# Differential attention in a hybrid trunk layer: queries and keys transposed once in fp32, duplicated by on-chip transfers, and split after the transposition

## The chip, the cores and the metric

The kernel runs on one core of a Trainium2 chip. The metric is the device time of one execution in microseconds. Five engines work side by side: TensorE (PE in the profile, its weight loads PEld), VectorE (DVE), ScalarE (ACT), GpSimd (POOL) and SyncE (SP), which here only issues transfers (DMAs). Each engine takes its instructions strictly in order, and an instruction that waits holds back everything behind it on its engine. [...]

## The reference, cut to what matters

One layer, 640 tokens (512 latent and 128 context tokens), width 1024: a SwiGLU half-step, then token mixing (differential attention beside an mLSTM), then a second half-step. The attention has 8 heads. Each has two components `c` of 64 features for queries and keys and 128 features for values:

```python
dq = rmsnorm(dq.reshape(B, T, DA_HEADS, 2, DA_HEAD_DIM), p['g_qn'][l])
dk = rmsnorm(dk.reshape(B, T, DA_HEADS, 2, DA_HEAD_DIM), p['g_kn'][l])
q_att = rope_2d(dq)
keys = jnp.concatenate([rope_2d(dk), k_ctx.astype(dk.dtype)], axis=1)
s = jnp.einsum('bqhcd,bkhcd->bhcqk', qi.astype(jnp.float32), kf) * scale
pr = jax.nn.softmax(s, axis=-1)
w = pr[:, :, 0] - lam * pr[:, :, 1]
return jnp.einsum('bhqk,bkhv->bqhv', w, vf)
```

The latent queries see 512 latent keys and 256 cached ones, the context queries see the 128 context keys. Everything is fp32; the inputs are given and the result is compared in fp32.

## The kernel before, in words

**Split products.** TensorE multiplies fp32 data in a faster reduced format, `float32r`. To keep the precision, every operand is split into a high part (the value rounded to `float32r`) and a low part (the value minus the high part), and products of high and low are summed. The high part is a Copy on ACT (`act`, line 51), the low part a subtraction on DVE (`tt`, line 54).

**The scores of a head.** A query component has only 64 features, so a contraction over 128 partitions has room for two copies. The query operand `qT` holds for each component the high part on one half of the partitions and the low part on the other half. The key operands `kH` and `kL` hold the high and the low part of the keys, the same on both halves. Then `qT` times `kH` plus `qT` times `kL` is the full product (`Head.scores`, line 708). The cached keys come from HBM in this layout already (`ck`, lines 1698 to 1700) and are only split.

**Getting there, before.** After the projections queries and keys lie token-major (`q_tok`, `k_tok`: 128 tokens on the partitions, 5 blocks of tokens), and the features have to come onto the partitions. `pack_queries` (1664) splits token-major into slots of 64 columns (high 0, low 0, low 1, high 1) in `qpk`, with one ACT and one DVE instruction; `pack_keys` (1672) lays the high part of the keys out twice in `kpk` with two ACT instructions. `queries` (1689) then turns `qpk` with ten TensorE transpositions (5 blocks by 2 components, `turn_features`, line 1679, through the `float32r` identity `identr`), which ACT copies from PSUM into `qT`; it makes the low part of the keys, also twice, in `kp2` (two DVE subtractions) and loads and splits the cached keys. `keys(0)` turns `kpk` (ten more, emptied by DVE), `keys(1)` turns `kp2` (ten more, emptied by ACT). So a head takes 30 transpositions, and the 8 heads take 240.

**Order of the work.** TensorE runs in program order (`mm`, `tr`, lines 74 to 78). Inside `with written()` ACT and DVE instructions are chained in the order written; all others, and the transfers issued by `nc.sync.dma_start`, are placed by a planner that simulates the timeline. Between the steps of a head, `fill.units(n)` puts projection work on TensorE. Such a unit is 24 matmuls of 256 columns or, in heads 1 to 5, half of a wide pair: 12 matmuls of 512 columns, two units after each other into the one PSUM bank `wide` (line 1366, `bufs=1`), which ACT empties with two instructions after the second half. The other PSUM tiles share four banks, tag `mm`. A head has ten such units, so the halves fall alike in each wide head: the last three units before the next head are a second half, a first half and a second half.

**A head in the loop** (lines 2103 to 2154). For each block of queries `qi` = 0 to 4: `scores(qi)`, `turn(qi-1)` (transposes the softmax weights, `ps_wT`), `soft(qi)` (two Exp on ACT), one unit, `mix(qi)` (DVE), `values(qi-1)` (`ps_o`), perhaps a second unit. At `qi == 3` the next head is packed. After the last block: `turn(4)`, `N.queries()`, a unit, `H.values(4)`, `finish_norm` (normalises the head's output), `N.keys(0)`, a unit, `N.keys(1)`, `fill.ahead()` (loads and begins to split a later granule of weights), a unit; then the next head. `H.finish` (transposes the output, `ps_aT`, in fp32 through `ident`, and stores it) runs inside the next head. Before head 0 the same steps run between eleven units (2068 to 2081), followed by `gate_rows` (1428), which prepares the mLSTM gates and stores two tiles `QA`, `QB` that `gate_load` and `gate_cols` (1509, 1512) bring back during head 1.

**Buffers.** The tag `pk` (two buffers of 5 KB a partition) holds rope scratch, `qpk`, `kpk` and `kp2`; the tag `asq` (one buffer of 2.5 KB) holds `ck`, `asq`, `aT` and `QQ`.

Of the kernel before, what the change touches and what calls it, by code (L numbers as in the profile page):

```python
# [18 lines left out]
NS = 512  # L19
# [12 lines left out]
def tile_trunk(ctx: ExitStack, tc: tile.TileContext, a: dict):  # L32
# [17 lines left out]
    def act(*args, **kw):  # L50
        return placed(nc.scalar.activation(*args, **kw))  # L51
# [1344 lines left out]
    mix = ctx.enter_context(ExitStack())  # L1396
    gq_p = mix.enter_context(tc.tile_pool(name="mlgate", bufs=1))
    ident = load(gq_p, [128, 128], a["ident"], name="ident")
    identr = gq_p.tile([128, 128], F32R, name="identr")
    vec.tensor_copy(identr, ident)  # L1400
    cols = gq_p.tile([128, 5, 4, 8], F32, name="cols")
    decay = gq_p.tile([128, 64, 5], F32, name="decay")

# [24 lines left out]
    def gate_rows(gt, ps):  # L1428
        b_g, m0 = of_rows

        def row(name):
            return gt.tile([64, T], F32, name=name)

        fg, ig = row("fg"), row("ig")
        for hf in range(2):
            cs = half(hf)
            p = ps[:, 512 * hf : 512 * hf + HALF]
            act(fg[:, cs], p[0:64], AF.Identity, bias=b_g[0:64])
            act(ig[:, cs], p[64:128], AF.Identity, bias=b_g[64:128])
# [12 lines left out]
        yield  # L1452
        tt(vec, u, ig, b, ALU.subtract)

        A, M = keep, lf
        vec.memset(A, 0.0)
        vec.tensor_copy(A[0:32, 128:512:128], b[0:32, 127:511:128])
        vec.tensor_copy(A[32:64, 127:511:128], b[32:64, 128:512:128])
        vec.memset(M, 0.0)
        yield  # L1460
        for d0, fl in ((0, False), (32, True)):
            r = slice(d0, d0 + 4)
            for c0, c1, init in ((0, 512, m0[r, 0:1]), (512, 640, 0.0)):
# [24 lines left out]

        yield
        QA = gt.tile([128, T], F32, name="QA")  # L1490
        QB = gt.tile([128, T], F32, name="QB")
        vec.tensor_copy(QA[0:64], u)

        def r3(t):
            return t.rearrange("p (c t) -> p c t", c=5)

        tt(vec, r3(e), r3(u), Ml[:, :, None].to_broadcast([64, 5, 128]), ALU.subtract)
        act(QA[64:128], e, AF.Exp)
        tt(vec, r3(ig), r3(nM), MP[:, :, None].to_broadcast([64, 5, 128]), ALU.add)
        act(QB[0:64], ig, AF.Exp)  # L1500
        tt(vec, b, nM, b, ALU.subtract)
        ts(b, b, 87.0, ALU.min)
        act(QB[64:128], b, AF.Exp)
        nc.sync.dma_start(out=qq_dram[:, 0, :], in_=QA)
        nc.sync.dma_start(out=qq_dram[:, 1, :], in_=QB)

    Q_at = [None]

# [145 lines left out]
    class Head:  # L1654
# [2 lines left out]
            self.pr, self.h = divmod(hd, 2)  # L1657
            self.s = {}

        def pack(self):  # L1660
            self.pack_queries()
            self.pack_keys()

        def pack_queries(self):

            hs = slice(self.h * 128, (self.h + 1) * 128)
            qv = q_tok[self.pr][:, :, hs].rearrange("p t (c d) -> p t c d", c=2)
            self.qpk = ap.tile([128, 5, 4, 64], F32R, tag="pk", name="qpk", bufs=2)
            act(self.qpk[:, :, 0::3, :], qv, AF.Copy)
            tt(vec, self.qpk[:, :, 1:3, :], qv, self.qpk[:, :, 0::3, :].bitcast(F32), ALU.subtract)  # L1670

        def pack_keys(self):
            hs = slice(self.h * 128, (self.h + 1) * 128)
            kv = self.kv = k_tok[self.pr][:, :, hs].rearrange("p t (c d) -> p t c d", c=2)
            self.kpk = ap.tile([128, 5, 4, 64], F32R, tag="pk", name="kpk", bufs=2)
            for i in range(2):
                self.at_act = act(self.kpk[:, :, i::2, :], kv, AF.Copy)

        def turn_features(self, pk, dst, key, ev):
            for i0, n in ((0, 2), (2, 2), (4, 1)):  # L1680
                p = psum.tile([128, 2, 2, 128], F32R, tag="mm", name="ps_qkT")
                for i in range(n):
                    flat = pk[:, i0 + i].rearrange("p s d -> p (s d)")
                    for c in range(2):
                        tr(p[:, c, i, :], flat[:, 128 * c : 128 * c + 128], identr)
                o = 768 if key and i0 == 4 else i0 * 128
                ev(dst[:, :, o : o + n * 128].rearrange("p c (i t) -> p c i t", i=n), p[:, :, :n, :].bitcast(F32))

        def queries(self):
            self.qT = ap.tile([128, 2, T], F32R, tag="qT", name="qT")  # L1690
            self.kH = ap.tile([128, 2, 896], F32R, tag="kH", name="kH")
            self.kL = ap.tile([128, 2, 896], F32R, tag="kL", name="kL")
            self.ao = ap.tile([128, 5, 128], F32, tag="ao", name="ao")
            self.turn_features(self.qpk, self.qT, False, lambda o, i: setattr(self, "at_q", act(o, i, AF.Copy)))
            self.kp2 = ap.tile([128, 5, 4, 64], F32R, tag="pk", name="kp2", bufs=2)
            for i in range(2):
                self.at_vec = tt(vec, self.kp2[:, :, i::2, :], self.kv, self.kpk[:, :, i::2, :].bitcast(F32), ALU.subtract)
            ck = load(ap, [128, 2, 256], a["cache_kd"][:, self.hd], tag="asq", name="ck")
            act(self.kH[:, :, 512:768], ck, AF.Copy)
            tt(vec, self.kL[:, :, 512:768], ck, self.kH[:, :, 512:768].bitcast(F32), ALU.subtract)  # L1700

        def keys(self, part):
            if part == 0:
                self.turn_features(self.kpk, self.kH, True, lambda o, i: vec.tensor_copy(o, i))
            else:
                self.turn_features(self.kp2, self.kL, True, lambda o, i: act(o, i, AF.Copy))

        def scores(self, qi):
            s = ps_s.tile([128, 1536], F32, tag="sc", name="sc")
# [358 lines left out]
    heads[0].pack()  # L2068
    fill.units(3)
    heads[0].queries()  # L2070
    fill.units(2)
    heads[0].keys(0)
    fill.units(2)
    heads[0].keys(1)
# [7 lines left out]
    def aside(hd, qi, part):  # L2082
# [7 lines left out]
                rotate()  # L2090
        elif qi != 3:
            rotate()
        if part == 1 and hd == 1 and qi in (1, 2):
            gate_load(qi - 1)
        if part == 0 and hd == 1 and qi in (2, 3):
            gate_cols()

    two, one = (1, 1), (1, 0)
# [4 lines left out]
    for hd in range(8):  # L2103
        H = heads[hd]
        odd = hd % 2
        for qi in range(5):
            n = UNITS[hd][qi]
            with written():
# [14 lines left out]
            if qi == 3 and hd < 7:  # L2123
                while odd and rotate():
                    pass
                with written():
                    heads[hd + 1].pack()
            aside(hd, qi, 1)
            if (hd, qi) == (0, 2):
                begin_pools()  # L2130
# [8 lines left out]
        with written():  # L2139
            H.turn(4)  # L2140
        if hd < 7:
            N = heads[hd + 1]
# [563 lines left out]
```

## Time and profile before

| | |
|---|---|
| device time, median of 3 runs | 1804.94 us (1804.79 to 1805.13) |
| the profiled execution: its time, and its span from first to last instruction | 1804.37 us, 1802.4 us |
| TensorE busy | 1778.2 us, 99% of the span |
| DVE busy, ACT busy | 1349.6 us (75%), 899.0 us (50%) |
| granted TensorE clock | 1.000 |
| the attention, head 0's first unit to the last head's end | about 654 to 1056 us |
| in that stretch: TensorE, DVE, ACT busy; DMA share | 398.7, 277.7, 228.4 of 402.1 us; 0.27 |
| one wide head (2 to 5) | 45.8 to 45.9 us |

How to read it: times are microseconds from the start of the span. A busy TensorE is not one at its peak, since matmuls overlap: the next one starts before the last one has ended. What an instruction costs TensorE is therefore the distance from its start to the next start, and not its duration. In a timeline row the number behind the start is the duration of the whole group, `xN` the instructions in it, and brackets show idle time of that engine ahead of it with what ended it. Names of tiles have their buffer numbers left out; all ACT instructions of the helper carry line 51, all DVE subtractions line 54, the transpositions line 78.

### The profile page before, as it was taken

The page shows a single profiled execution, that of the slowest core. Times are in us where ns is not written, and L with a number is a line of the kernel's source. Part 1 is how long each engine was busy: PE and PEld are TensorE (multiplying, and loading weights), DVE is VectorE, ACT ScalarE, POOL GpSimd, SP SyncE. Part 2 cuts the span into 40 slices and gives each one's busy share as a digit, 9 for nine tenths or more (in the row PEclk, how much of TensorE's full clock was granted, in tenths as well). Part 3 has the DMA queues.
Part 4 walks back from the last instruction along what each step waited for, and adds up shares of the span by engine and source line. Part 5 has one row for each costly group of instructions (what it writes and reads, how often), then busy time and mean ns, then how long its engine had stood idle before and what let it go on. Part 6 is the DMA issues. An engine that isn't in the chain of part 4 may idle for free.

```text
span 1802.4 us, 29657 instructions
## 1 busy us (share of the span) xinstructions
PE 1778.2 (99%) x11950; PEld 1712.3 (95%) x11950; DVE 1349.6 (75%) x2162; ACT 899.0 (50%) x1579; POOL 40.8 (2%) x72
## 2 busy tenths in 40 slices
PE   8999999999999999999999999999999999999998
PEld 6999999999999999888889998899999999999998
DVE  6879887576888858777775637876768888896485
ACT  5654544332655556565655546562326545544432
POOL 0000000100000000000000000000000000000010
PEclk9999999999999999999999999999999999999999
DMA  8364565978235543222222335665642455557992
GB/s 330 110 199 162 193 241 205 360 220 279 90 120 194 187 147 96 78 72 75 72 87 98 111 121 196 201 245 190 227 164 77 143 167 190 207 176 274 355 311 82
DMA packets 144923, 317.85 MB, mean 176 GB/s; under 512 B 10577, under 2 KB 106577, under 8 KB 133009
## 3 DMA queue, kind: packets, MB, share of 16 engines
q1 hardware_dynamic: 133410, 270.20, 43.7%
q0 software_dynamic: 10688, 43.13, 7.4%
q10 hardware_dynamic: 688, 2.63, 0.4%
q8 instruction: 94, 1.54, 0.3%
q14 instruction: 43, 0.35, 0.1%
HBM read 243.77 MB, written 72.15 MB: 175 GB/s over the span
## 4 chain that ended last, share of the span: by engine, by line
PE 85%; DVE 7%; DMA 4%; ACT 2%; issue 1%; SPq 0%; ACTq 0%; DVEq 0%
PE ps_f L75 48%; PE ps_p L75 15%; PE ps_t L75 10%; PE sc L75 3%; PE ps_o L75 2%; PE ps_n L75 2%; DVE ww L54 2%; DMA raw_a<-in_w_ada_k 1%; PE ps_wT L78 1%; PE ps_u L75 1%; PE ps_qkT L78 1%; DMA raw<-in_w2b 1%; DVE junk L814 1%; DMA a_raw<-aT_dram 1%; DMA P<-nm_dram 1%
## 5 line engine op out<-in xcount | busy, mean ns | idle before, releaser
L75 PE MATMUL ps_f<-S,ww 128*128 128x320 f32 x2400 | 387.2, 309 | 4.4 <-ACT u L51 1.9
L75 PEld LDWEIGHTS ps_f<-S,ww 128*128 128x128 f32 x2400 | 359.7, 188 | 8.7 <-DVE ww L54 4.6
L54 DVE TENSOR_TENSOR ww<-raw,ww 128x2048 fp32r<-128x2048 f32 (+1 forms) x73 | 163.9, 2245 | 66.0 <-ACT ww L51 65.9
L75 PE MATMUL ps_f<-hm,ww 128*128 128x320 f32 x1176 | 185.7, 309 | 0.1
L75 PEld LDWEIGHTS ps_f<-hm,ww 128*128 128x128 f32 x1176 | 175.7, 188 | 0.4 <-DVE ww L54 0.3
L51 ACT ACTIVATE ww<-raw 128x2048 fp32r<-128x2048 f32 (+1 forms) x73 | 136.8, 1875 | 59.7 <-DVE raw L54 40.3
L54 DVE TENSOR_TENSOR raw<-raw 128x1024 f32<-128x1024 f32 x186 | 160.8, 864 | 2.4
L75 PE MATMUL ps_f<-hm,wB 128*128 128x320 f32 x1008 | 161.5, 309 | 0.0
L75 PE MATMUL ps_t<-wH,hH 128*128 128x256 f32 (+1 forms) x440 | 151.6, 345 | 1.0 <-DVE x L57 0.9
L75 PE MATMUL ps_p<-hH,wH 128*128 128x320 f32 x480 | 150.9, 314 | 1.6 <-DVE num L54 1.6
L75 PEld LDWEIGHTS ps_f<-hm,wB 128*128 128x128 f32 x1008 | 151.3, 188 | 0.0
L75 PE MATMUL ps_p<-hH,wL 128*128 128x320 f32 x480 | 148.3, 309 | 0.0
L75 PE MATMUL ps_p<-hL,wH 128*128 128x320 f32 x480 | 148.3, 309 | 0.0
L75 PE MATMUL ps_t<-wH,hL 128*128 128x256 f32 (+1 forms) x440 | 146.4, 333 | 0.9 <-DVE hL L54 0.9
L75 PE MATMUL ps_t<-wL,hH 128*128 128x256 f32 (+1 forms) x440 | 146.3, 333 | 0.0
L51 ACT ACTIVATE u<-ps_f 128x320 f32<-128x320 f32 x129 | 55.7, 432 | 154.6 <-PE ps_f L75 154.5
L54 DVE TENSOR_TENSOR wL<-raw,wH 128x2048 fp32r<-128x2048 f32 x37 | 84.6, 2288 | 25.9 <-ACT wH L51 25.9
L51 ACT ACTIVATE wH<-raw 128x2048 fp32r<-128x2048 f32 (+1 forms) x45 | 75.4, 1681 | 49.7 <-PE ps_p L75 40.3
L54 DVE TENSOR_TENSOR wB<-raw,wB 128x1024 fp32r<-128x1024 f32 x64 | 78.0, 1219 | 26.6 <-ACT wB L51 26.6
L814 DVE CUSTOM_DVE_ANT_0 junk<-raw_a,csil 128x1024 bf16<-128x1024 f32 (+1 forms) x76 | 92.6, 1218 | 2.1 <-DMA raw_a<-in_w_ada_c 1.6
L75 PEld LDWEIGHTS ps_t<-wH,hL 128*128 128x128 f32 x440 | 83.6, 190 | 9.8 <-DVE hL L54 1.1
L75 PEld LDWEIGHTS ps_t<-wH,hH 128*128 128x128 f32 x440 | 83.5, 190 | 9.4 <-ACT nsq L51 1.1
(311 smaller groups left out, 3569.7 us busy)
## 6 DMA issues: line engine op xcount, KB each, us to landing
g_dram<-g SPq DMA_DIRECT2D x44, 640.0 KB, 7.5
raw_a<-in_w_ada_c POOLq DMA_DIRECT2D x38, 512.0 KB, 5.1
g_dram<-g SPq DMA_DIRECT2D x24, 480.0 KB, 8.6
raw<-in_w1b SPq DMA_DIRECT2D x11, 1024.0 KB, 4.9
raw<-in_w3b SPq DMA_DIRECT2D x11, 1024.0 KB, 6.4
raw<-in_w1a SPq DMA_DIRECT2D x10, 1024.0 KB, 4.9
raw<-in_w3a SPq DMA_DIRECT2D x10, 1024.0 KB, 6.2
hm<-g_dram SPq DMA_DIRECT2D x7, 1280.0 KB, 13.3
```

The source lines that it names most:

```text
L51: return placed(nc.scalar.activation(*args, **kw))
L54: return placed(eng.tensor_tensor(out=out, in0=in0, in1=in1, op=op))
L75: tc.keep_in_program_order(nc.tensor.matmul(*args, **kw))
L78: tc.keep_in_program_order(nc.tensor.transpose(*args, **kw))
L814: placed(vec.tensor_tensor_reduce(out=junk, in0=raw, in1=self.csil[:, v, :], op0=ALU.mult, op1=ALU.add, scale=1.0, scalar=0.0, accum_out=m ...
```

## The change

Queries and keys are turned once, whole and unsplit, in fp32. `turned` replaces the packing and `turn_features`: five transpositions through the fp32 identity `ident` for a head's 128 columns (both components together: component 0 lands on partitions 0 to 63, component 1 on 64 to 127), in two PSUM tiles, which ACT copies into an SBUF tile `t`. Four transfers from SBUF to SBUF then write each component's 64 partitions onto both halves of a tile `both` (160 KB each, 64 partitions by 2560 bytes, all issued by SP). Only then is the data split, feature-major: `queries` copies all of `qd` into `qT` as the high part and overwrites partitions 64 to 127 with the low part; `keys` makes `kH` and `kL` from the cached keys (part 0), the latent keys (1) and the context keys (2).

```diff
-    identr = gq_p.tile([128, 128], F32R, name="identr")
-    vec.tensor_copy(identr, ident)
...
+        def turned(self, tok):
             hs = slice(self.h * 128, (self.h + 1) * 128)
+            t = ap.tile([128, T], F32, tag="asq", name="qk_t")
+            for i0, n in ((0, 4), (4, 1)):
+                p = psum.tile([128, 4, 128], F32, tag="mm", name="ps_qkT")
                 for i in range(n):
+                    tr(p[:, i, :], tok[:, i0 + i, hs], ident)
+                act(t[:, i0 * 128 : (i0 + n) * 128], p.rearrange("p a b -> p (a b)")[:, : n * 128], AF.Copy)
+            both = ap.tile([128, 2, T], F32, tag="pk", name="qk_d", bufs=2)
+            for r in range(2):
+                for c in range(2):
+                    nc.sync.dma_start(out=both[64 * r : 64 * r + 64, c, :], in_=t[64 * c : 64 * c + 64])
+            return both
+        def turn_queries(self):
+            self.qd = self.turned(q_tok[self.pr])
+        def turn_keys(self):
+            self.kd = self.turned(k_tok[self.pr])
+        def load_cache(self):
+            self.ck = load(ap, [128, 2, 256], a["cache_kd"][:, self.hd], tag="ck", name="ck")
...
+            self.at_q = act(self.qT, self.qd, AF.Copy)
+            r = slice(64, 128)
+            tt(vec, self.qT[r], self.qd[r], self.qT[r].bitcast(F32), ALU.subtract)
+        def keys(self, *parts):
+            for n in parts:
+                c0, c1 = ((512, 768), (0, 512), (768, 896))[n]
+                v = (self.ck, self.kd[:, :, 0:NS], self.kd[:, :, NS:T])[n]
+                act(self.kH[:, :, c0:c1], v, AF.Copy)
+                self.at_vec = tt(vec, self.kL[:, :, c0:c1], v, self.kH[:, :, c0:c1].bitcast(F32), ALU.subtract)
```

In the loop the steps lie so. At `qi == 3`, where the next head was packed, its queries are turned; at `qi == 4`, behind `values(3)`, its keys. After `turn(4)` come `N.queries()` and `N.keys(0)`, a unit, `H.values(4)`, `N.keys(1, 2)`, then `finish_norm` and the other two units with no transposition between them. All these are now inside `written()`, except that the transfers are placed by the planner.

```diff
                 with written():
-                    heads[hd + 1].pack()
+                    N.turn_queries()
+                N.load_cache()
+            if qi == 4 and hd < 7:
+                with written():
+                    N.turn_keys()
...
-            N.queries()
+            with written():
+                N.queries()
+                N.keys(0)
             fill.units(n[0])
             with written():
                 H.values(4)
+                N.keys(1, 2)
             H.finish_norm()
-            N.keys(0)
             fill.units(n[1])
-            N.keys(1)
```

Ahead of head 0 the two turns come first, then three units, `queries`, `keys(0, 1, 2)`, four units, and the rest as before. Three smaller edits go with it: `ck` gets a buffer of its own and `asq` is used by `t` instead; `gate_rows` works in place and stores four half tiles instead of `QA` and `QB`; and `gate_load` and `gate_cols` move from head 1 to heads 2 and 4, since they use `asq`.

More of the change, by code (lines that the diff above doesn't have):

```diff
@@ L1489, in gate_rows @@
         yield
-        QA = gt.tile([128, T], F32, name="QA")
-        QB = gt.tile([128, T], F32, name="QB")
-        vec.tensor_copy(QA[0:64], u)
         def r3(t):
             return t.rearrange("p (c t) -> p c t", c=5)
+        nc.sync.dma_start(out=qq_dram[0:64, 0, :], in_=u)
         tt(vec, r3(e), r3(u), Ml[:, :, None].to_broadcast([64, 5, 128]), ALU.subtract)
-        act(QA[64:128], e, AF.Exp)
+        act(e, e, AF.Exp)
+        nc.sync.dma_start(out=qq_dram[64:128, 0, :], in_=e)
         tt(vec, r3(ig), r3(nM), MP[:, :, None].to_broadcast([64, 5, 128]), ALU.add)
-        act(QB[0:64], ig, AF.Exp)
+        act(ig, ig, AF.Exp)
+        nc.sync.dma_start(out=qq_dram[0:64, 1, :], in_=ig)
         tt(vec, b, nM, b, ALU.subtract)
         ts(b, b, 87.0, ALU.min)
-        act(QB[64:128], b, AF.Exp)
-        nc.sync.dma_start(out=qq_dram[:, 0, :], in_=QA)
-        nc.sync.dma_start(out=qq_dram[:, 1, :], in_=QB)
+        act(b, b, AF.Exp)
+        nc.sync.dma_start(out=qq_dram[64:128, 1, :], in_=b)
     Q_at = [None]
@@ L1658, in __init__ @@
             self.s = {}
[L1660 to L1664, printed above, removed]
+        def turned(self, tok):
             hs = slice(self.h * 128, (self.h + 1) * 128)
[L1667 to L1681, printed above, removed]
-                for i in range(n):
[L1683 to L1687, printed above, removed]
+            t = ap.tile([128, T], F32, tag="asq", name="qk_t")
@@ L1693, in queries @@
             self.ao = ap.tile([128, 5, 128], F32, tag="ao", name="ao")
[L1694 to L1706, printed above, removed]
+            self.at_q = act(self.qT, self.qd, AF.Copy)
[7 more added lines that the diff above has]
+                self.at_vec = tt(vec, self.kL[:, :, c0:c1], v, self.kH[:, :, c0:c1].bitcast(F32), ALU.subtract)
         def scores(self, qi):
@@ L2067, in tile_trunk @@
     gt = gates.enter_context(tc.tile_pool(name="gates", bufs=1))
-    heads[0].pack()
+    heads[0].load_cache()
+    heads[0].turn_queries()
+    heads[0].turn_keys()
     fill.units(3)
     heads[0].queries()
[L2071 to L2074, printed above, removed]
+    heads[0].keys(0, 1, 2)
+    fill.units(4)
     with tc.issue_after(heads[0].at_vec.ins), tc.issue_after(heads[0].at_q.ins):
@@ L2092, in aside @@
             rotate()
-        if part == 1 and hd == 1 and qi in (1, 2):
-            gate_load(qi - 1)
-        if part == 0 and hd == 1 and qi in (2, 3):
+        if (qi, part) == (1, 1) and hd in (2, 4):
+            gate_load(hd // 2 - 1)
+        if (qi, part) == (2, 0) and hd in (2, 4):
             gate_cols()
@@ L2105, in tile_trunk @@
         odd = hd % 2
+        N = heads[hd + 1] if hd < 7 else None
         for qi in range(5):
@@ L2141, in tile_trunk @@
         if hd < 7:
-            N = heads[hd + 1]
-            N.queries()
+            with written():
+                N.queries()
+                N.keys(0)
             fill.units(n[0])
```

## The prediction

> **What bounds the kernel now.** I read the page first, then busy time by stage, then TensorE's timeline where one head hands over to the next.
>
> ```profile
> span 1802.4 us, 29657 instructions
> ...
> PE 1778.2 (99%) x11950; PEld 1712.3 (95%) x11950; DVE 1349.6 (75%) x2162; ACT 899.0 (50%) x1579; POOL 40.8 (2%) x72
> ...
> PE 85%; DVE 7%; DMA 4%; ACT 2%; issue 1%; SPq 0%; ACTq 0%; DVEq 0%
> ...
> 825.80:871.70 45.90, 45.80 (x267) 39.22 (x266) 31.39 (x47) 26.47 (x57) 0.00 (x0) 1.00 0.24 74
> ...
> 653.90:1056.00 402.10, 398.73 (x2650) 362.41 (x2649) 277.66 (x423) 228.44 (x477) 0.00 (x0) 1.00 0.27 87
> 1056.00:1250.00 194.00, 190.30 (x1168) 177.93 (x1167) 136.45 (x394) 106.02 (x265) 2.65 (x5) 1.00 0.60 208
> ```
>
> TensorE bounds the whole program and this stage too: 398.73 of 402.10 us in the attention. The third and fourth busy times of a stage row are DVE and ACT, and both have room. So what shortens TensorE's row of starts shortens the time, unless a wait takes the place. The end of head 3 (wide units) shows the row:
>
> ```profile
> 853.34 1.50 PE L75 MATMUL ps_o<-v_tok,wT 128*128 128x128 f32 x12
> 854.60 0.36 PE L75 MATMUL sc<-kH,qT 128*128 128x256 f32 x1
> ...
> 859.18 1.50 PE L75 MATMUL ps_o<-v_tok,wT 128*128 128x128 f32 x12
> 860.51 0.27 PE L78 MATMUL ps_wT<-ident,p 128*128 128x128 f32 x1
> 860.54 1.05 PE L78 MATMUL ps_qkT<-identr,qpk 128*128 128x128 f32 x10
> 861.42 0.46 PE L75 MATMUL ps_t<-wH,hH 128*128 128x512 f32 x1
> ...
> 864.03 0.39 PE L75 MATMUL ps_t<-wH,hL 128*128 128x512 f32 x1
> 864.26 0.38 PE L75 MATMUL ps_o<-v_tok,wT 128*128 128x128 f32 x2
> 864.40 1.05 PE L78 MATMUL ps_qkT<-identr,kpk 128*128 128x128 f32 x10
> 865.28 0.46 PE L75 MATMUL ps_t<-wH,hH 128*128 128x512 f32 x1
> ...
> 868.11 0.96 PE L78 MATMUL ps_qkT<-identr,kp 128*128 128x128 f32 x10
> 868.91 0.46 PE L75 MATMUL ps_t<-wH,hH 128*128 128x512 f32 x1
> ...
> 871.75 0.39 PE L75 MATMUL sc<-kH,qT 128*128 128x512 f32 x1
> ...
> 875.94 0.71 PE L78 MATMUL ps_aT<-ident,ao 128*128 128x128 f32 x5
> 876.41 0.48 PE L75 MATMUL ps_t<-wH,hH 128*128 128x512 f32 x1
> ```
>
> **Removed: 30 transpositions a head.** From start to next start the three groups take 861.42 − 860.54 = 0.88, 865.28 − 864.40 = 0.88 and 868.91 − 868.11 = 0.80, so 2.56 us a head and 20.5 us for eight.
>
> **Added: 10 transpositions a head in fp32.** The row for five fp32 transpositions of this shape is `ps_aT`: 876.41 − 875.94 = 0.47 us. Two groups make 0.94 us a head, 7.5 us in all. Net on TensorE: −13.0 us.
>
> **Given back: the bank of the wide units.** In heads 1 to 5 the first unit after `turn(4)` ends a wide pair, and the next one needs the same single bank. ACT empties it thus:
>
> ```profile
> 861.12 1.36 ACT L51 ACTIVATE qT<-ps_qkT 128x512 fp32r<-128x512 f32 x3
> 864.46 0.38 ACT L51 ACTIVATE k_tok<-ps_t 128x256 f32<-128x256 f32 x1 [1.97 <-PE ps_t L75]
> 864.74 0.38 ACT L51 ACTIVATE q_tok<-ps_t 128x256 f32<-128x256 f32 x1
> ```
>
> The pair ends at 864.03 + 0.39 = 864.42, the bank is empty at 864.74 + 0.38 = 865.12, and the next unit can start near 865.16. Before, the ten `kpk` transpositions fill just that time. After the change only `ps_o` (0.14 us) lies there, so the unit would be ready at 864.40 and waits 0.76 us. Five such places: +3.8 us. This assumes that ACT is free then. In `written()` order ACT has the two copies of the turned keys (0.60 and 0.28), `wT`, the Copy into `qT` (1.27) and the cached keys (0.64) ahead, 3.1 us, less the overlaps between neighbours; counted from X, the start of the keys' transpositions (860.4 on the clock above, where `ps_o` of block 3 is through), they run from X + 0.6 to about X + 3.5. The pair ends at X + 0.47 + 0.10 (`wT`) + 2.84 (a unit, 861.42 to 864.26) + 0.16 (its last matmul's overhang, 864.42 − 864.26) = X + 3.6. It fits, barely.
>
> ```profile
> L51 ACT ACTIVATE wT<-ps_wT 128x512 f32<-128x512 f32 x32 | 19.1, 597 | 52.8 <-PE ps_wT L78 52.6
> ...
> L51 ACT ACTIVATE wT<-ps_wT 128x128 f32<-128x128 f32 x8 | 2.2, 278 | 18.9 <-PE ps_wT L78 18.9
> ...
> L51 ACT ACTIVATE rope<-k_tok 128x1280 f32<-128x1280 f32 x3 | 3.8, 1273 | 0.0
> ...
> L51 ACT ACTIVATE kH<-ck 128x512 fp32r<-128x512 f32 x8 | 5.1, 638 | 1.0 <-DMA ck<-in_cache_kd 0.7 <-PE sc L75 0.3
> ...
> L51 ACT ACTIVATE rope<-k_tok 128x1024 f32<-128x1024 f32 x3 | 3.2, 1069 | 0.9 <-DVE k_tok L54 0.9
> ...
> L54 DVE TENSOR_TENSOR k_tok<-k_tok,rope 128x1024 f32<-128x1024 f32 x3 | 3.7, 1219 | 0.0
> ...
> L54 DVE TENSOR_TENSOR k_tok<-k_tok,qky 128x1280 f32<-128x1280 f32 x3 | 4.5, 1492 | 0.1
> ```
>
> **Covered: stalls at `qi == 4`.** TensorE now waits there, in most heads, for the mixed weights of block 3 and for a bank behind the packing on ACT (waits in us in total, times, longest):
>
> ```profile
> PEld ps_wT L78 <- DVE p L57: 2.1, 6, 0.9
> ...
> PEld ps_t L75 <- ACT stage L51: 1.0, 4, 0.3
> ...
> PEld ps_t L75 <- ACT q_tok L51: 0.5, 2, 0.3
> ```
>
> The queries' transpositions (0.47 us) come to lie ahead of `scores(4)`, the keys' ahead of `turn(4)`, so the first 2.1 us are work instead of waiting; and ACT has 0.9 us of copies at `qi == 3` where it had three packings, so I take 1 of the other 1.5. Together −3 us (bounds: 0 and −3.6).
>
> **The transfers.** No row of the trace shows one from SBUF to SBUF, or on 64 partitions. Nearest rows, with the KB moved and the median from issue to landing:
>
> ```profile
> mq_dram<-stage SPq DMA_DIRECT2D x9, 160.0 KB, 1.9
> ...
> mkT<-mk_dram SPq DMA_DIRECT2D x2, 640.0 KB, 3.9
> ...
> mqT<-mq_dram SPq DMA_DIRECT2D x1, 640.0 KB, 8.9
> ...
> 881.31 0.33 SPq L97 DMA_DIRECT2D ck<-in_cache_kd  x1
> ```
>
> Let L be the time from the first issue of a turn to its last landing. Issues take 0.33 us each. Four transfers side by side give 3 × 0.33 + 1.9 = 2.9; 640 KB as one gives 3.9; bounds 2.9 and 8.9; I take 3.9, the same bytes on an idle queue. The stage uses 0.27 of the DMA engines, and at this boundary SP issues little else. The keys' `t` is ready at X + 0.6 + 0.9, so they land at X + 1.6 + L = X + 5.5. `kH` takes ACT 1.07 and `kL` DVE 1.22 us: ready at X + 7.9 with the semaphores. TensorE reaches the next `scores(0)` at X + 3.6 + 0.7 + 2 × 2.84 = X + 10.0. Hidden, with 2 us to spare; its cover is the two units behind `values(4)`. The single `asq` buffer is a second limit: the keys' copy at X + 0.6 needs the queries' transfers out of it, which start about 4.5 us before X: turned behind `ps_o` of block 2 at 854.6, copied until 855.9. With L = 3.9 that holds too.
>
> [...]
>
> ACT and DVE otherwise lose work: DVE gives up `qpk`, `kp`, and the emptying of `kH`, ACT the packings and two emptyings of `ps_qkT`; what they gain is the six rows above and a 1.5 us subtraction for `qT`. I cost this at nothing; TensorE's units hide it. So too the gate stores and the moved `gate_load`.
>
> **Ahead of head 0.** The removed groups lie there too. New: the four `mm` banks all go to the turns at once, and ACT has this in front:
>
> ```profile
> 654.00 1.92 ACT L51 ACTIVATE wH<-raw 128x2048 fp32r<-128x2048 f32 x1 [1.06 <-PE ps_f L75]
> 655.82 0.41 ACT L51 ACTIVATE g_out<-ps_f 128x320 f32<-128x320 f32 x1
> ```
>
> The transpositions would end near 654.9, and the first copy starts at 655.9, so the first unit gets its bank at 655.9 + 0.6 = 656.5: +1.6 us (0 if the planner puts the copies first, +4 if the banks of the last gate products and the keys' copy come late as well).
>
> **Sum.** −13.0 + 3.8 − 3.0 + 1.6 = −10.6 us. 1804.37 − 10.6 = 1793.8 on the profiled execution's time, which is 0.57 below the median of the runs: 1794.3 us. With the bounds of the terms this case spans 1790 to 1799.
>
> **Rivals.** (a) *More of it arrives*: the wide bank or the start costs nothing. Without the +3.8 and the +1.6: about 1789. For it: the planner may order anew; against it: the bank's row is firm.
>
> (b) *ACT is held by the keys' transfer; slower.* If the planner expects the keys' landing before the wide pair's end, it puts their Copy into `kH` ahead of the two copies that empty the bank. Then ACT stands until X + 5.5, copies 1.07, empties 0.66: the unit starts at X + 7.2 instead of X + 4.3, 2.9 us at five places, 14.5 us: 1808.8. It eats the gain from L = 3.1 on. For it: planned order and real order differ; against it: the ACT row is full until the pair ends, so a landing before X + 3.5 has to be expected.
>
> (c) *The four transfers run one behind another*: L = 4 × 1.9 = 7.6. Then the queries leave `asq` only at X + 3.1, the keys land at X + 3.1 + 1.0 + 7.6 = X + 11.7 and `kL` is ready at X + 14.1, so `scores(0)` waits 4.1 us at seven boundaries: +29, 1823. It loses from L = 6.3 on. [...]
>
> (d) *Nothing arrives*: what the attention saves is waited for later, since the stages behind it run with twice its DMA share. Time 1804. Against it: the chain gives DMA 4%.
>
> **How the numbers follow.** The forecast 0.50, (a) 0.14, (b) 0.17, (c) 0.13, (d) 0.06. About 0.2% (3.6 us) is what a measurement of this kernel can tell from no change. Faster: the forecast, (a), and 0.04 of (b) with a small L: 0.68. Same: (d) and 0.04 of (b): 0.10. Slower: the rest of (b), 0.09, and (c): 0.22. The range takes in (a), the forecast, (d) and (b): 1788 to 1811; (c) and some edge are left out. The likeliest case's own range is 1790 to 1799.
>
> **What would show it.** `ps_qkT` shrinks to 80 transpositions, five in about 0.47 us. In heads 1 to 5 TensorE waits some 0.8 us between `ps_o` of block 4 and the next unit, released by ACT's `q_tok` or `stage` copy; under (b) several us, and ACT's `kH` idle before it on a DMA. Landing medians of the new transfers near 3 us for a single one and 4 for a turn confirm L; `sc` of block 0 waiting for DVE `kL` shows (c). Wrong in the whole it is if TensorE's idle time in the attention, now 3.4 us, grows by more than 13.

## The result and the profile after

| kernel | device time, median (range), us | ratio to before, 95% interval |
|---|---|---|
| before | 1805.04 (1804.08 to 1807.33, 6 runs) | |
| changed | 1817.35 (1815.94 to 1823.29, 6 runs) | 1.0069 [1.0054, 1.0084] |

The change makes the kernel 12.3 us slower; the prediction was 10.6 us faster. The profiled execution of the changed kernel, 1823.29 us, is the slowest of its six, and 6.2 us of its excess lie ahead of the attention (the last gate product starts at 660.02 in place of 653.80), where the program is the same; two stretches at half the TensorE clock, at 36 and 391 us, lie there (granted clock 0.50 from 36.0 to 39.4 and from 391.0 to 394.4 us; 1.00 in the same windows before), and the profile before has none. So the stages are compared and not the spans. The page of the changed kernel (busy time, share, instructions; then the chain that ended last):

```profile
span 1821.5 us, 29435 instructions
...
PE 1776.0 (98%) x11790; PEld 1706.8 (94%) x11790; DVE 1340.9 (74%) x2136; ACT 892.9 (49%) x1563; POOL 40.8 (2%) x72
...
PE 79%; DVE 9%; DMA 7%; ACT 3%; issue 1%; SPq 1%; ACTq 0%; DVEq 0%
```

Every engine has less to do, and yet DMA and DVE have a larger share of the chain. The attention, from the start of the last gate product to the scores of the last head's block 4, before (window, its length, then TensorE, weight loads, DVE, ACT busy, clock, DMA share):

```profile
653.80:1049.85 396.05, 393.86 (x2616) 357.97 (x2614) 273.60 (x416) 225.89 (x470) 0.00 (x0) 1.00 0.27 86
```

and after:

```profile
660.02:1067.49 407.47, 387.74 (x2456) 350.45 (x2454) 264.95 (x391) 221.15 (x457) 0.00 (x0) 0.99 0.36 109
```

The stage is 407.47 − 396.05 = 11.4 us longer. TensorE is busy for 6.1 us less, but idle for 407.47 − 387.74 = 19.7 us in place of 2.2. That the busy time fell by 6.1 and not by 13.0 is mostly the clock, which was halved in three stretches of 3.4 us (below), about 1.7 us each. What TensorE waited for in the attention before (us in total, times, longest):

```profile
PE ps_wT L78 <- DVE p L57: 1.5, 3, 0.7
PE sc L75 <- ACT p L51: 1.1, 1, 1.1
PE ps_o L75 <- ACT wT L51: 0.5, 1, 0.5
```

and after:

```profile
PE ps_aT L78 <- DVE ao L54: 8.4, 5, 2.6
PE ps_t L75 <- ACT stage L51: 3.9, 5, 1.2
PE ps_o L75 <- ACT wT L51: 2.9, 2, 2.4
PE sc L75 <- ACT p L51: 1.8, 1, 1.8
PE ps_qkT L78 <- ACT g_out L51: 1.6, 1, 1.6
PE ps_t L75 <- ACT q_tok L51: 1.1, 2, 0.5
```

These are idle times between the ends that the profile models; counted from start to start, as the prediction counts, such a wait comes out some 0.2 us longer, since matmuls overlap (the wide bank at head 3's end: 0.53 us idle, 0.77 from start to start). The largest is new and stands in no part of the prediction: `ps_aT`, the transposition of a head's output, which TensorE does one unit into the *next* head, waits for `ao`. Head 3's end shows how it comes about. TensorE:

```profile
877.26 0.71 PE L78 MATMUL ps_qkT<-ident,k_tok 128*128 128x128 f32 x5
877.80 0.27 PE L78 MATMUL ps_wT<-ident,p 128*128 128x128 f32 x1
...
880.67 0.38 PE L75 MATMUL ps_o<-v_tok,wT 128*128 128x128 f32 x2
881.58 0.50 PE L75 MATMUL ps_t<-wH,hH 128*128 128x512 f32 x1 [0.53 <-ACT q_tok L51]
...
887.15 0.39 PE L75 MATMUL sc<-kH,qT 128*128 128x512 f32 x1
...
892.54 0.76 PE L78 MATMUL ps_aT<-ident,ao 128*128 128x128 f32 x5 [1.04 <-DVE ao L54]
```

ACT in the same stretch:

```profile
881.15 0.38 ACT L51 ACTIVATE q_tok<-ps_t 128x256 f32<-128x256 f32 x1
883.49 1.37 ACT L51 ACTIVATE kH<-qk_d 128x1024 fp32r<-128x1024 f32 x2 [1.96 <-DMA qk_d<-qk_t]
884.76 0.72 ACT L51 ACTIVATE asq<-ao 128x640 f32<-128x640 f32 x1
885.39 1.90 ACT L51 ACTIVATE wH<-raw 128x2048 fp32r<-128x2048 f32 x1
887.19 0.19 ACT L51 ACTIVATE rt<-rv 128x5 f32<-128x5 f32 x1
```

and DVE:

```profile
884.58 1.56 DVE L54 TENSOR_TENSOR kL<-qk_d,kH 128x1024 fp32r<-128x1024 f32 x2 [2.04 <-ACT kH L51]
886.06 0.81 DVE L1762 TENSOR_REDUCE ass<-asq 128x5 f32<-128x640 f32 x1
...
887.32 2.29 DVE L54 TENSOR_TENSOR wL<-raw,wH 128x2048 fp32r<-128x2048 f32 x1 [0.24 <-ACT wH L51]
889.53 0.16 DVE L57 SCALAR_TENSOR_TENSOR rt<-ry 128x5 f32<-128x5 f32 x1
889.60 1.75 DVE L1716 TENSOR_REDUCE mn<-sc 128x2 f32<-128x1536 f32 x1
...
891.66 0.82 DVE L54 TENSOR_TENSOR ao<-ao,ry 128x640 f32<-128x640 f32 x1
```

ACT stands 1.96 us for the keys' landing. Behind its `kH` copy, in order, stands the Square of `finish_norm` (`asq<-ao`), ready to run since 882.6, when `ao` of block 4 was written; it also needs the buffer `asq`, which the keys' turned tile holds until its transfers have been read. So it starts at 884.76. By then `wH` and `wL` (1.90 and 2.29 us) and the next head's `mn` (1.75) come between the steps of `finish_norm`, and `ao` is done at 891.66 + 0.82 = 892.48, 5.3 us after the scores of the next head began. The keys themselves are in time: `kL` ends at 884.58 + 1.56 = 886.14, the scores start at 887.15 without a wait.

At the end of head 0 the buffer itself holds ACT. Behind the queries' transfers, which land late there, stands the copy of the turned keys, and behind that copy the `wT` of block 4, for which TensorE waits 2.4 us ahead of `ps_o`:

```profile
736.33 0.77 ACT L51 ACTIVATE qk_t<-ps_qkT 128x512 f32<-128x512 f32 x2 [4.83 <-DMA qk_d<-qk_t]
```

SP's row for the four transfers of head 3's end (from SBUF, the working memory, to SBUF):

```profile
878.74 2.38 SPq L1668 DMA_DIRECT2D qk_d<-qk_t  x4
```

and the page's group of all of them (KB each, median us from issue to landing):

```profile
qk_d<-qk_t SPq DMA_DIRECT2D x64, 160.0 KB, 2.9
```

Four issues take 2.38 us, 0.60 each, and the last lands 2.9 us after its own: L = 3 × 0.60 + 2.9 = 4.7 us, as the 4.75 from 878.74 to 883.49 say.

That is 0.8 us more than the 3.9 that the forecast used. Of the 4.7 us, 1.8 is the pace of the issues; whether the transfers also wait for one another, no run here shows.

### The profile page after: what moved, and what is told of

The parts are those of the page before. It is cut to its first block, busy times and chain, and to the rows that moved or that the text cites. A ratio compares the mean times of both kernels' runs of the same rounds, so it can differ in the third digit from the quotient of the medians.

```text
span 1821.5 us, 29435 instructions
## 1 busy us (share of the span) xinstructions
PE 1776.0 (98%) x11790; PEld 1706.8 (94%) x11790; DVE 1340.9 (74%) x2136; ACT 892.9 (49%) x1563; POOL 40.8 (2%) x72
## 4 chain that ended last, share of the span: by engine, by line
PE 79%; DVE 9%; DMA 7%; ACT 3%; issue 1%; SPq 1%; ACTq 0%; DVEq 0%
PE ps_f L75 48%; PE ps_p L75 14%; PE ps_t L75 7%; PE sc L75 2%; PE ps_o L75 2%; DVE ww L54 2%; DMA qk_d<-qk_t 2%; PE ps_n L75 1%; DMA raw_a<-in_w_ada_k 1%; DMA P<-nm_dram 1%; DVE wL L54 1%; PE ps_wT L78 1%; DMA raw<-in_w2a 1%; DMA raw<-in_w2b 1%; DVE mn L1716 1%
```

## The experiments

**One lock or two.** Is `finish_norm` late for the buffer, for the order, or does neither help, since the transfers or DVE are the limit?

*own*: the keys' turned tile gets another place.

```diff
-            t = ap.tile([128, T], F32, tag="asq", name="qk_t")
+            t = ap.tile([128, T if tag == "asq" else 768], F32, tag=tag, name="qk_t")[:, :T]
...
-            self.kd = self.turned(k_tok[self.pr])
+            self.kd = self.turned(k_tok[self.pr], "p1")
```

> Edit: only the keys' turned tile (qk_t of turn_keys) changes its place, from the single buffer asq to the single buffer p1, which is idle between mix of group 4 and the next soft. So at the end of head 0 ACT needn't stand for the queries' transfers before it empties the keys' transposition bank. Theory 1 (the lateness of finish_norm has two locks, the buffer asq held by the keys' transfers and the order on ACT, where the Square stands behind the kH copies that wait for the landing): the stall of 2.58 us ahead of ps_o(4) of head 0 goes, with the half-rate stretch of 3.41 us behind it (about 1.7 us), and the waits of ps_aT for ao (1.34, 1.24, 2.64, 1.20, 2.77 us, together 9.2) stay, since the order on ACT is the same: 1817.4 - 4.3 = about 1813. Theory 2 (the buffer alone is the lock): the waits of ps_aT go too, 1817.4 - 13.5 = about 1804. Theory 3 (the transfers themselves are too slow, whatever the buffers): no change, 1817.

Measured: 1813.05 us (1811.07 to 1815.68), ratio to before 1.005 [1.0038, 1.0063]. The number is that of theory 1, though its interval overlaps with the changed kernel's, and only half of its reason holds. What TensorE waited for:

```profile
PE ps_aT L78 <- DVE ao L54: 7.2, 4, 2.6
...
PE sc L75 <- ACT kH L51: 2.0, 1, 2.0
...
PE sc L75 <- DVE kL L54: 0.5, 1, 0.5
PE sc L75 <- ACT p L51: 0.5, 1, 0.5
```

The waits of `ps_aT` stay, as theory 1 says: with the order unchanged, the free buffer is of no use to the Square. But the stall at the end of head 0 didn't go; it moved, from `ps_o` (2.9 us in two waits after the change, one of 0.5 now) to the scores of head 1 (2.0 + 0.5), since the transfers still landed late there (6.5 us in the median from 700 to 742 us). What went is at the start of head 0: the scores' wait for ACT's `p` fell from 1.8 to 0.5 us. There the copy of the turned keys came 6.1 us behind that of the queries in the changed kernel (668.96 and 662.87), for `asq`; in this run both are one group.

*first*: the order alone; `finish_norm` is written ahead of the keys, and its sum on DVE (`ass`) is chained in the written order with the rest.

```diff
                 H.values(4)
-                N.keys(1, 2)
-            H.finish_norm()
+                H.finish_norm()
+                N.keys(1, 2)
```

> Edit: only the order; finish_norm is written ahead of keys(1, 2), so that its Square and its DVE steps stand ahead of kH(keys), kL(keys), wL and mn on both engines. The buffer asq is still the one of the keys' turned tile. Theory 1 (two locks): the Square still can't start before the keys' transfers have been read (883.5 in head 3's end, against 884.76), but all behind it follows at once: ao is done near 883.5 + 0.7 + 0.6 + 0.9 + 0.6 + 0.8 = 887 in place of 891.7, so the waits of ps_aT (together 9.2 us) go; kL(keys) follows ao and ends 1 to 3 us later than 886.1, where the scores of group 0 began at 887.15, so that up to 2 us a head comes back there in 7 heads: 1817.4 - 9.2 + (0 to 14), most likely about 1814. Theory 2 (the buffer alone): ACT stands for the buffer with kH behind it, and nothing is gained: 1817 or more. Theory 3 (DVE as a whole is full at the change of heads): what ps_aT gains, the scores lose, about 1817 to 1820.

Measured: 1816.68 us (1813.28 to 1817.33), 1.0064 [1.0052, 1.0077]. No gain that the ranges can tell from 1817.35. TensorE's first wait in this kernel is

```profile
PE sc L75 <- DVE kL L54: 5.5, 7, 1.1
```

and none for `ao` is left. Most of the 8.4 us went to the scores, once in each of seven heads, as theory 1 had it: with `asq` still locked, the Square waits for the keys' transfers, and then `kL` waits for `finish_norm`. ACT at the end of head 3:

```profile
875.65 0.74 ACT L51 ACTIVATE asq<-ao 128x640 f32<-128x640 f32 x1 [2.08 <-DMA qk_d<-qk_t]
```

*own_first*: both.

> Both edits of the two runs before together: the keys' turned tile in p1, and finish_norm written ahead of keys(1, 2). Theory 1: the Square starts when ao of group 4 is written (about 881.7 in head 3's end), ao is done near 885, kL(keys) starts when kH has been copied and ao is done and ends near 887, about when the scores want it. The five waits of ps_aT (9.2 us) and the stall of head 0 with its half-rate stretch (4.3 us) go, the scores lose at most 1 us a head: 1817.4 - 13.5 = 1804, 1802 to 1808, and the sum of the gains of the two single edits is less than this one's. Theory 3 (transfers or DVE as a whole): 1810 or more.

Measured: 1804.8 us (1803.47 to 1808.03, 11 runs), 1.0001 [0.999, 1.0011]. The 4.3 and 0.7 us of the single edits make 12.6 together (by the ratios to before: 3.4, 0.9 and 12.3). Two locks, each of which hides the other: theory 1. ACT, and then DVE, at the end of head 3:

```profile
869.98 0.74 ACT L51 ACTIVATE asq<-ao 128x640 f32<-128x640 f32 x1 [1.05 <-DVE ao L61]
...
872.20 1.06 ACT L51 ACTIVATE kH<-qk_d 128x1024 fp32r<-128x1024 f32 x1
```

```profile
872.90 0.83 DVE L54 TENSOR_TENSOR ao<-ao,ry 128x640 f32<-128x640 f32 x1
873.64 1.55 DVE L54 TENSOR_TENSOR kL<-qk_d,kH 128x1024 fp32r<-128x1024 f32 x2
```

The Square now runs while the keys are on their way, and `kH` has no wait on a transfer left here. At the end of head 0 it still has one: the scores of head 1 wait 3.4 us for `kH`.

**What the transfers cost in all.** *nodma*, the changed kernel with its orders and buffers, without the transfers:

```diff
-            for r in range(2):
-                for c in range(2):
-                    nc.sync.dma_start(out=both[64 * r : 64 * r + 64, c, :], in_=t[64 * c : 64 * c + 64])
+            for c in range(2):
+                placed(vec.tensor_copy(both[:, c, :], t))
```

> Edit, on the changed kernel itself (orders and buffers as the change has them): the four transfers of a turn are left out; two copies on DVE from the turned tile to the two places take their place. This leaves out of the computation that each component is laid on both halves of the partitions (each half keeps its own), so the scores are of other numbers; every other instruction and operand shape is the same, and DVE has about 1 to 1.5 us more in a turn. It tells what the transfers' latency costs in all. Theory 1 (the loss is the landing of the transfers, 4.75 us a turn, passed on through ACT's order and the buffer asq to ao and ps_aT): kH of the keys is copied some 3 us earlier, the Square behind it too, and the waits of ps_aT, at the end of head 0 and at its start go, together about 9.2 + 4.3 + 3: 1817.4 - 16.5 = 1801, 1799 to 1805. Theory 2 (the order on ACT and DVE with kH and kL ahead of finish_norm is the loss, whatever the transfers take): ps_aT goes on waiting for ao, 1812 or more.

Measured: 1802.22 us (1800.48 to 1805.37), 0.999 [0.9982, 0.9999]. The transfers' latency costs the changed kernel 1817.35 − 1802.22 = 15.1 us (14.3 by the ratios), though DVE copies 0.9 us more in each turn. Theory 1 holds, with a remainder for theory 2:

```profile
PE ps_t L75 <- ACT stage L51: 4.0, 3, 1.4
PE ps_aT L78 <- DVE ao L54: 3.6, 2, 1.8
PE ps_t L75 <- ACT q_tok L51: 2.7, 2, 1.4
```

In two heads `ps_aT` waits even now, behind `wL`, `mn` and a part of the rotation of `k_tok` on DVE (the added copies may have a share; no run separates it). And the keys, ready early, are copied into `kH` ahead of the emptying of the wide bank, so that TensorE idles 1.3 to 1.4 us there in each of the five wide heads instead of 0.53: the mechanism of rival (b), at a small price.

**The start.** *start*:

```diff
     heads[0].turn_queries()
+    fill.units(1)
     heads[0].turn_keys()
-    fill.units(3)
+    fill.units(2)
```

> Edit: one of the three units ahead of queries() is moved between the turning of the queries and of the keys of head 0, so that the keys' transpositions don't wait for their bank while ACT empties g_out. If the lag of 3.4 us at the start (first unit 9.6 us later than before where the last landmark ahead of it was 6.2 later) is that wait of 1.8 us for ACT with the half-rate stretch behind it, this gains 1.8 to 3.5 us: 1814 to 1815.5. If the lag comes from the profiled execution alone, or if the wait goes to the next unit's bank or to queries(), it gains nothing: 1817.

Measured: 1817.35 us (1812.87 to 1818.42), 1.0068 [1.0056, 1.0081]: no change. The wait for `g_out` (1.6 us) is now the unit's; it meets whatever asks for the third bank. Most of the rest of the 3.4 us was a stretch at half rate (last section) in the profiled execution of the changed kernel, at a granted clock of 0.50 from 664.10 to 667.40 us; the mean clock of that execution is 0.995, that of this run's 0.998.

**Head 0's end.** *early0*, on top of own_first: head 1's queries and keys are turned at blocks 1 and 2, and its turned keys lie in `asq` again.

```diff
-            if qi == 3 and hd < 7:
+            if qi == (3 if hd else 1) and hd < 7:
...
-            if qi == 4 and hd < 7:
+            if qi == (4 if hd else 2) and hd < 7:
```

> Edit, on top of own_first: during head 0 the queries and keys of head 1 are turned two groups of queries earlier (groups 1 and 2 in place of 3 and 4; head 1 takes them from the tokens that head 0 has, so they are there), and both use the buffer asq. In own_first the scores of head 1 wait 3.5 us for qT and kH and 1.0 us for kL, with a stretch at half rate behind them, because its eight transfers land 7.1 us after their issue behind 2 MB of raw weights. Theory A (it is this one meeting of transfers with weight loads): the 4.5 us go, with up to 1.7 us of half rate: 1804.8 - 6 = about 1799, at least 1801. Theory B (it is ACT and DVE at the end of head 0, not the transfers): the scores of head 1 wait as long as before, 1805.

Measured: 1800.94 us (1799.39 to 1804.45, 11 runs), 0.9987 [0.9977, 0.9996], 0.13% below before, with an interval just clear of 1. Against own_first the medians differ by 3.9 us and the ratios by 2.5, with intervals that overlap; neither is 6. In own_first's profile the scores of head 1 wait 3.4 us for `kH`, and the granted clock from 656 to 1050 us is 0.99 (1.00 in early0's); in the runs bank and gates, which are the same up to there, they wait only 0.5, and the landing of the transfers differs with it (median 7.1 us in own_first, 5.5 in bank and gates, 2.8 in early0, from 700 to 742 us). The meeting with the weight loads is real, but its price changes from execution to execution.

**What takes the place of a removed wait.** *bank*, on top of own_first:

```diff
-                at[0] = wide_ps[0].tile([128, 512], F32, tag="wide", name="ps_t")
+                at[0] = (psum if i == 4 else wide_ps[0]).tile([128, 512], F32, tag="mm" if i == 4 else "wide", name="ps_t")
```

> Edit, on top of own_first: the last of every five wide projections takes its PSUM bank from the pool of four in place of the one wide bank, so that the unit behind ps_o(4) needn't wait until ACT has emptied the wide bank (0.69 us in each of heads 1 to 5, 3.45 us together). Theory A (the wait is a cost of its own): 1804.8 - 3.45 = 1801.4. Theory B (at the end of each head the keys are the path: kL of the keys begins at 873.64 in head 3's end, the scores reach it at 874.9 and wait 0.12 us): the 0.69 us come back as waits of the scores for kL, since nothing ahead of kL moves: 1804 to 1805.

Measured: 1804.1 us (1799.88 to 1807.19), 1.0 [0.999, 1.001]: theory B. The five waits are gone and the scores wait instead, where own_first has 0.5 us once:

```profile
PE sc L75 <- DVE kL L54: 4.2, 6, 0.8
```

*gates*, on top of own_first: `gate_load` and `gate_cols` in head 1 again, as before the change.

> Edit, on top of own_first: the loading and turning of the gate rows goes back to head 1 (groups 1 to 3), as before the change; the buffer asq is free there now. Theory A (the waits of 1.13 and 1.12 us between ps_wT and ps_t in heads 2 and 4 come from the gate rows' turning there): they go, 1804.8 - 2.3 = about 1802.5, and a new wait of at most 0.5 us may come in head 1. Theory B (they come from the order on ACT, where rope and wH stand ahead of the emptying of the wide bank in every even head whatever the gate rows do): 1804.5 to 1805.5.

Measured: 1803.15 us (1800.54 to 1806.25), 0.9996 [0.9987, 1.0005], not to be told from own_first. TensorE's waits on `q_tok` and `stage` are the same as in own_first (2.0 us in 3, 2.5 in 4): theory B, ACT's order.

*best*: early0, bank, gates, and two more orders.

```diff
+            self.keys(0)
             self.at_q = act(self.qT, self.qd, AF.Copy)
...
                 H.finish_norm()
                 N.keys(1, 2)
+                H.finish_scale()
```

(`finish_scale` is the last multiplication of `finish_norm`.)

> Edits of early0, bank and gates together, on top of own_first, and two more on the order at the end of a head: the split of the cached keys stands ahead of queries() (so that DVE doesn't hold ao of group 4 behind qT and kL of the cache, 1.3 us), and the last multiplication of finish_norm (ao, 0.82 us) stands behind kL of the keys. If theory B of bank holds, these two move kL of the keys up by 0.5 to 0.8 us and so let the 0.69 us of the bank be gained. Sum: 1804.8 - 6 (head 0) - 3.4 (bank) - 2.3 (gates) = 1793, 1791 to 1798, and so below the kernel before. If what is left at the heads' ends is the time of the transfers themselves, about 1797 to 1800.

Measured: 1801.17 us (1799.03 to 1804.93), 0.9987 [0.9978, 0.9995], the same as early0 alone. The sum of single gains, 1793, failed: the scores wait for `kL` in five heads (1.2 us), and the wait for `wT` grew from 0.5 to 1.9 us.

Three more on top of early0. *early_start* puts a unit ahead of head 0's queries:

```diff
+    fill.units(1)
     heads[0].turn_queries()
+    fill.units(1)
     heads[0].turn_keys()
-    fill.units(3)
+    fill.units(1)
```

> Edit, on top of early0: at the start of the attention one projection unit goes ahead of the turning of head 0's queries, one between queries and keys, one behind. In early0 the keys' transpositions wait 1.80 us and the first unit 0.40 us for banks that ACT empties late (g_out behind a wH of 1.9 us). In the run start, with the queries' turning first, the same wait went to the unit. Theory A (with a unit of 2.9 us ahead, the banks are empty by the time they are asked for): 2.2 us go, 1800.9 - 2.2 = 1798.7. Theory B (the wait is for the banks of the stage before and meets whatever comes third): it stays, 1801.

Measured: 1806.05 us (1803.85 to 1813.39), 1.0014 [1.0005, 1.0023]. The waits for the banks went, as in theory A, and yet it is some 5 us slower than early0. The later queries moved `gate_rows` back on DVE (its `lf` starts at 678.11 and not at 669.96), and at their end an ACT instruction of these rows stands ahead of the scores' `p`:

```profile
690.06 0.74 ACT L51 ACTIVATE e<-e 64x640 f32<-64x640 f32 x1 [9.82 <-DVE e L54]
691.67 0.90 ACT L51 ACTIVATE p<-sc,mn 128x768 f32<-128x768 f32 x1 [0.87 <-DVE mn L1716]
```

TensorE waits 6.6 us for that `p`. Neither theory had it.

*tail* is early_start with the edits of best except that of gates.

> Edit: early_start with the bank, the split of the cached keys ahead of queries(), and the last multiplication of finish_norm behind kL of the keys (the edits of best without that of gates). In best the five waits for the wide bank (3.44 us) had gone, and the scores waited 0.36 to 0.48 us a head for kL in their place, 0.4 us were lost elsewhere, and at groups 1 and 2 ACT's order cost 0.9 us in heads 2 and 4. Theory A (the waits of best in heads 2 and 4 came with the gate rows' going back): 1798.7 - 1.3 = 1797.4. Theory B (ACT is the limit at these places, and what TensorE gains at a head's end it loses within two groups): no gain, 1798.7.

Measured: 1806.11 us (1805.11 to 1807.55), 1.001 [1.0002, 1.0019]: no gain, theory B.

*late_wh*, on top of tail, moves one copy of 1.9 us on ACT:

```diff
                 H.soft(qi)
+                if qi == 1 and hd in (1, 3, 5):
+                    fill.ahead()
```

> Edit, on top of tail: in heads 1, 3 and 5 the copy wH of 1.9 us that ACT makes between groups 0 and 1 is written behind the two exponentials of group 1, so that it no longer stands ahead of k_tok and q_tok, which empty the wide bank. Theory A (the wait of 1.1 us ahead of the unit of group 1 in heads 3 and 5 is this order on ACT): 2.2 us go, tail - 2.2. Theory B (wH is then late for the projections or stands ahead of another copy): the same or slower than tail.

Measured: 1823.23 us (1821.89 to 1823.95), 1.0106 [1.0091, 1.012]: 17 us worse, theory B and more. DVE in head 3:

```profile
851.35 2.29 DVE L54 TENSOR_TENSOR wL<-raw,wH 128x2048 fp32r<-128x2048 f32 x1 [3.75 <-ACT wH L51]
853.56 0.16 DVE L1731 RECIPROCAL rc<-sm 128x2 f32<-128x2 f32 x1
```

The `wL` written ahead of the mixing now waits for the later `wH`, and `rc`, `r` and `p`, which TensorE wants, stand behind it: TensorE waits 3.1 to 3.9 us for `p` in three heads. That is the fault of the change over again: a wait on one engine holds what stands behind it, and that is what the next engine needs.

## Why the prediction was wrong

**TensorE's side was right.** Five transpositions of `ps_qkT` take 877.80 − 877.26 = 0.54 us to the next start, predicted 0.47. The busy time fell by 6.1 us, and with the three half-rate stretches put back (3 × 1.7) by some 11, predicted 13.0.

**The wide bank was right as a wait** (idle 0.53 us at each of five places; at head 3's end 881.58 − 880.67 − 0.14 = 0.77 us from start to start, predicted 0.76) and wrong as a term of its own: bank shows that the time behind it is the keys' anyway, once `finish_norm` stands ahead of them.

**The start was right within its bounds**: idle 1.6 us ahead of the keys' transpositions and 0.2 ahead of the first unit, about 2.2 from start to start; predicted 1.6, bounds 0 to 4. No order tried took it away for less than it cost.

**The stalls at `qi == 4`** went, but alike waits came elsewhere: `ps_wT` still waits 0.7 us for `p`, and `ps_t` 1.2 us for `stage` in each of heads 2 and 4. Of the −3 little arrived.

**L was mis-sized**: 3.9 predicted, 4.7 measured. The issues take 0.60 us and not 0.33, which is 0.8 us in three of them. The keys' landing came at X + 6.2 (predicted 5.5), `kL` at X + 8.9 (7.9), the scores at X + 9.9 (10.0). Even so they were in time, and rival (c) fell, with no scores waiting for `kL` in the changed kernel. Rival (b) didn't happen either: `k_tok` and `q_tok` were emptied ahead of `kH`. But its sign came in, `kH` idle on ACT for a DMA (1.96 us): it had the right engine and the right wait, and the wrong consumer. Rivals (a) and (d) didn't happen.

**The step that failed** is "ACT and DVE otherwise lose work ... I cost this at nothing; TensorE's units hide it." Busy time fell on both, but order was what mattered. I followed the keys' landing to the scores, found two microseconds to spare, and stopped there. I didn't list what stands behind the waiting `kH` copy on ACT, and who waits for that: the Square, the other steps of `finish_norm`, `ao`, `ps_aT`. These have a due time too, one unit into the next head, and `ps_aT` was even among the quoted rows, as a price for a transposition. With it goes the sentence on `asq`, "With L = 3.9 that holds too": it asked only whether the keys' copy finds the buffer free, not whether the next user, the Square, does, and not what 2 MB of weight loads in front do to L at the end of head 0. There and at head 0's start ACT stood for that buffer, and the waits of `ps_o` for `wT` and of the scores for `p` grew by 2.4 and 0.7 us.

So of the 22.9 us between −10.6 and +12.3, 15.1 go when the transfers are left out (nodma), and 12.6 go with the transfers in place when the two locks are undone (own_first). A part is the clock, for which the prediction has no term: (1 − granted clock) times the span is 5.7 us in the mean of the changed kernel's six runs, 1.3 to 1.7 for before in the experiments and 1.6 in nodma. By this estimate about 4 us of the 12.3, and as much of the 15.1, are lost at half clock; that this lies behind the new waits is read from single profiles (last section), not shown run by run. The other 7.8 us are the difference between nodma and the forecast. Its rows show 3.6 at `ps_aT` and 2.9 at the wide bank (4.0 + 2.7, predicted 3.8), and of the stalls' −3.0 only 1.9 arrived there (the three rows before sum to 3.1, and 1.2 of such waits are left). That is 7.6; these are rows of single profiles, so the sum fits but is no proof of each term.

My own sign of failure, idle time of TensorE growing by over 13 us, came in: it grew by 19.7 − 2.2 = 17.5.

## What to carry to other kernels

When a wait is put on an engine that takes its work in order (here ACT, which stood 1.96 us for the keys' landing, with the Square behind it), list what stands behind it until the wait's latest end, and follow each of these to its consumer and its due time; that the data waited for arrives in time says nothing of the rest. Look at every later user of a buffer that a transfer reads, not just at the next one. Where two locks hold the same step, undoing one shows little (own and first: 4.3 and 0.7 us; both: 12.6), and a single edit without gain doesn't acquit its cause.

## What the runs showed of the hardware

**The transfers from SBUF to SBUF on 64 partitions are dear to issue.** 160 KB take SP 0.60 us in place of the 0.33 us that the load of a head's cached keys takes in the row that the prediction quotes (0.35 in the median after), and land after 2.9 us in the median, after 6.6 at most in the attention.

**TensorE's clock was halved behind three waits of 1.64 to 2.42 us.** The changed kernel's stretches (same columns as above, the granted clock third from the end):

```profile
664.10:667.40 3.30, 3.30 (x18) 3.30 (x17) 1.30 (x5) 0.00 (x0) 0.00 (x0) 0.50 0.91 285
...
701.70:704.90 3.20, 3.20 (x16) 3.20 (x16) 3.17 (x4) 2.38 (x5) 0.00 (x0) 0.50 0.17 24
...
739.30:742.50 3.20, 3.20 (x17) 3.20 (x16) 2.44 (x3) 1.56 (x4) 0.00 (x0) 0.50 0.48 127
```

Each follows a wait of TensorE, idle for 1.64, 1.82 and 2.42 us, lasts 3.41 us (from 664.08, 701.62 and 739.17 us on) and costs about half of that. Idle times of 2.48 and 2.62 us in the same execution had none behind them (granted clock 1.00 from 844 to 851 and from 939 to 946 us), so it depends on more than the wait's length. The wait of 1.6 us at the start stands in the profiles of early0 and best too, whose mean granted clock is 1.000, where one stretch of 3.41 us at 0.50 would by my estimate make it 0.999 (1.7 of some 1798 us). In own and own_first, where the scores of head 1 wait 2.0 and 3.4 us for `kH`, the granted clock from 656 to 1050 us is 0.99; in early0, where they don't wait for it, 1.00. What decides it besides the length, no run here shows. The six runs of the changed kernel have mean granted clocks of 0.995 to 0.998 and lie between 1815.94 and 1823.29 us. So single profiles of the same code differ by some microseconds.
